# A transposed tile of the first FFN: one staging buffer, or the spent buffer of its other factor

## The chip, the cores and the metric

The kernel runs on one core of a Trainium2 chip. A core has a matrix engine (TensorE, PE in the profile), VectorE (DVE), ScalarE (ACT), GpSimd (POOL) and SyncE (SP), which in this kernel only issues transfers. The engines run side by side, each through its own list of instructions in order, and wait for each other on semaphores. Transfers between the chip's main memory and the on-chip memory are done by 16 DMA engines; here they are issued by SP and, where the transfer adds to what lies in the buffer, by POOL. The metric is the time of the program on the device in microseconds, lower is better; a run here is one launch of the whole program.

## The reference

The program is one layer of a diffusion backbone: half-step SwiGLU feed-forward network (FFN), token mixing, second FFN, final norm. It takes 256 context tokens and 256 latent tokens of width 2048. The part in question is the first FFN, which both kinds of tokens pass:

```python
def half_step_ffn(x, mod, i, g, w_up, w_down):
    h = adaln(x, g, mod, i)
    a, b = jnp.split(h @ w_up, 2, axis=-1)
    return x + 0.5 * mod[:, i + 2, None, :] * ((jax.nn.silu(a) * b) @ w_down)
```

`silu(a) * b` is the gated hidden activation. It is 5632 wide and is computed in blocks of 512 columns.

## The kernel before

**Precision.** Products are made of three matmuls: each fp32 operand is split into a rounded half `hi` (ScalarE, line 128) and a remainder `lo` (VectorE, line 129), and `mm3` (line 152) multiplies hi by hi, lo by hi and hi by lo. Weights arrive as 1 MB tiles, 128 x 2048, each split in two halves of 1024 columns. There are four `hi` and four `lo` buffers, so at most two weight tiles stand ready ahead of TensorE.

**Blocks.** The 11 blocks of hidden columns (`NB` is 11) are numbered 0 to 10. Block 0 is done differently and is not touched. Blocks 1 to 10 are each done by one call of `quad(n)`, which is a product of 2 x 2 sub-matrices with seven products instead of eight (`order`, m = 0 to 6). Each product takes two weight tiles, q = 0 and 1: 14 steps to a block, 24 matmuls to a step. Weight tiles lie in `chain_[0]` and `chain_[1]`, which stay and to which POOL adds the next summand by an accumulating transfer (line 740), or in the three `raw` buffers, which SP loads.

**Gating.** A block makes four gated tiles of 128 x 512 fp32 (256 KB). For tokens s = 0 (context) and 1 (latent):

- `p1` and `c11` (m = 0, 1) put silu of the first factor into `ca[s]`; `ca` has two buffers.
- `kept` (line 872, m = 2) copies a partial sum from PSUM into `cy[s]`, two buffers; `p35` (line 876, m = 3) does so into `cb[s]`, tag `c12`, two buffers.
- `c12` (m = 4) completes `cb[s]`, multiplies `ca[s]` by it and appends the tile to the list `turn`.
- `c22` (m = 5) completes `cy[s]` and takes a new `ca[s]`; `c21` (m = 6) does silu in it, multiplies by `cy[s]` and appends that tile to `turn`.

So each product has two factors in two buffers: the result stands in `ca[s]`, and the other factor, in `cb[s]` or `cy[s]`, is not read again.

**Turning.** `turned()` takes one tile from the list `turn`: VectorE transposes it in blocks of 32 x 32 (line 842) from `ca` into the tile `stg` of the pool `chp`, of which there is one buffer, and SP stores `stg` to main memory, `hidd[n]` (line 844). It is called once in each m, after the first group of matmuls of q = 0. Tiles of m = 4 are thus turned in m = 5 and 6 of the same block, tiles of m = 6 in m = 0 and 1 of the next.

**The order.** The framework places the instructions on their engines with a planner that estimates times and frees buffers; instructions marked with `keep_in_program_order`, such as the transposes through `pinned`, keep the order in which they are written. Semaphore waits are put in by the framework. A new tile in a buffer waits for all readers of the old one, stores among them.

**Beside it.** A stream of conditioning weights (`side`) runs through VectorE in the same loop: 512 KB tiles `sraw`, two buffers, loaded by SP and reduced on VectorE (line 208) against vectors in `cBh`. `cBh` is loaded anew once on the way (line 203).

**The change of stage.** After block 10 the remaining tiles are turned. The pool `f1u`, which holds `cBh`, `sraw`, `ca`, `cy` and `c12`, closes, and `f1` opens in its place with the accumulator `acc`. The down-projection runs in `pair(p)`, p = 0 to 4, again with seven products. Its first results are copied by ScalarE from PSUM into `acc` (line 1078). The last tile, (10, 3), is not turned at once: `turned` puts it into `last_turn`, and `pair(0)` turns it in its second step (line 1152). Block 10 is read back only by the last pair. Later, `last1` uses the same buffer `stg` of `chp` for another purpose (line 1222).

Of the kernel before, what the change touches and what calls it, by code (L numbers as in the profile page):

```python
# [9 lines left out]
F32 = mybir.dt.float32  # L10
# [9 lines left out]
P = 128  # L20
# [26 lines left out]
CB = 512  # L47
# [11 lines left out]
def tile_layer(ctx: ExitStack, tc: tile.TileContext, I: dict, out: bass.AP):  # L59
    nc = tc.nc  # L60
# [12 lines left out]
    def bank():  # L73
        return ps["mm"].tile([P, 512], F32, tag="mm", name="mm")

    def tbank():
        return ps["tr"].tile([P, 512], F32, tag="tr", name="tr")
# [38 lines left out]
    def raw_tile(n=2048):  # L116
        t = wp.tile([P, 2048], F32, tag="raw", name="raw", bufs=3)
        return t if n == 2048 else t[:, :n]

    def split(raw, n=2048):  # L120

        half = n // 2
        parts = []
        for h in range(2):
            hi = wp.tile([P, 1024], F32R, tag="hi", name="hi", bufs=4)[:, :half]
            lo = wp.tile([P, 1024], F32R, tag="lo", name="lo", bufs=4)[:, :half]
            src = raw[:, h * half : (h + 1) * half]
            scalar[0].activation(hi, src, AF.Copy)  # L128
            vector[0].tensor_tensor(lo, src, hi.bitcast(F32), op=ALU.subtract)  # L129
            parts.append((hi, lo))  # L130

        def at(w):
            h, o = divmod(w.start, half)
            return tuple(x[:, o : o + w.stop - w.start] for x in parts[h])

        return at
# [11 lines left out]
    def mm3(out_ap, sh, sl, mh, ml, first, last, skip=False, still=False):  # L148

        rest = ((sh, ml), (sl, mh)) if still else ((sl, mh), (sh, ml))  # L150
        for n, (s, m) in enumerate(((sh, mh), *rest)):
            tensor[0].matmul(out_ap, s, m, start=first and not n, stop=last and n == 2, skip_group_check=skip)  # L152
# [541 lines left out]
    hidd = [dr.tile([4, P, CB] if n else [P, 16, P], F32, name=f"hid{n}") for n in range(NF // FB)]  # L694
# [18 lines left out]
    def pinned(ins):  # L713
        tc.keep_in_program_order(ins)
# [22 lines left out]
    chp = chcm.__enter__()  # L737
# [3 lines left out]
    with pool(name="f1u", bufs=1) as f1u:  # L741
# [7 lines left out]
        def ca_tile():  # L749
            return f1u.tile([P, CB], F32, tag="ca", name="ca", bufs=2)  # L750
# [9 lines left out]
        def part(n, ab, c):  # L760
            return I["w_up1b"][n - 1, ab, c]

        def first_chain(n, c):
            nc.sync.dma_start(chain_[c], part(n, 0, c))
# [64 lines left out]
        forms = token_forms()  # L829
        steps(forms, 2)  # L830
        turn = []
        last_turn = []

        def turned():

            if not turn:
                return
            n, t, ca = turn.pop(0)

            def staged():  # L840
                stg = chp.tile([P, CB], F32, tag="stg", name="stg")
                pinned(nc.vector.transpose(stg, ca))
                s, tt = divmod(t, 2)
                nc.sync.dma_start(hidd[n][2 * tt + s], stg)

            if (n, t) == (NB - 1, 3):
                last_turn.append(staged)
            else:
                staged()

        add = lambda o, x, y: nc.vector.tensor_tensor(o, x, y, op=ALU.add)
        negative = lambda o, y: nc.vector.scalar_tensor_tensor(o, o, -1.0, y, op0=ALU.mult, op1=ALU.mult)
# [1 line left out]
        def c12_tile():  # L854
            return f1u.tile([P, CB], F32, tag="c12", name="c12", bufs=2)

        def quad(n, after=lambda step: None):

            X, Y, Z = {}, {}, {}
            ca, cy, cb, ra = {}, {}, {}, {}  # L860

            def p1(s):
                ca[s] = ca_tile()
                nc.scalar.activation(ca[s], X[s], AF.Copy)

            def c11(s):
                add(ca[s], Z[s], ca[s])
                nc.scalar.activation(ca[s], ca[s], AF.Silu)

            def kept(s):  # L870
                cy[s] = f1u.tile([P, CB], F32, tag="cy", name="cy", bufs=2)
                nc.scalar.activation(cy[s], Y[s], AF.Copy)

            def p35(s):
                cb[s] = c12_tile()
                nc.scalar.activation(cb[s], Y[s], AF.Copy)

            def c12(s):
                add(cb[s], X[s], cb[s])
                negative(ca[s], cb[s])  # L880
                turn.append((n, 2 * s, ca[s]))

            def c22(s):
                add(cy[s], X[s], cy[s])
                ca[s] = ca_tile()
                nc.scalar.activation(ca[s], X[s], AF.Copy)

            def c21(s):
                add(ca[s], Y[s], ca[s])
                nc.scalar.activation(ca[s], ca[s], AF.Silu)  # L890
                negative(ca[s], cy[s])
                turn.append((n, 2 * s + 1, ca[s]))

            def chained(ab, c):
                return lambda q: accum(chain_[q], part(n, ab, c + q))

            def again(q):
                if n + 1 < NB:
                    first_chain(n + 1, q)
                else:  # L900
                    nc.sync.dma_start(chain_[q], I["w_dn1"][0, 2 * q])

            def loaded(q):
                ra[q] = raw_tile()
                nc.sync.dma_start(ra[q], part(n, 1, 2 + q))
                return ra[q]

            def plain(q):
                r = raw_tile()
                nc.sync.dma_start(r, part(n, 0, 2 + q))  # L910
                return r

            held = lambda q: chain_[q]
            order = (
                (a11, held, X, True, chained(1, 0), p1),
                (a12, plain, Z, True, None, c11),
                (n1, held, Y, True, chained(1, 2), kept),
                (s4, loaded, Y, False, lambda q: accum(ra[q], part(n, 1, q)), p35),
                (s2, held, X, False, chained(0, 2), c12),
                (s3, lambda q: ra[q], X, False, None, c22),  # L920
                (a22, held, Y, True, again, c21),
            )
            for m, (a, src, dst, fresh, then, use) in enumerate(order):
                if fresh:
                    dst.update({s: bank() for s in range(2)})
                for q in range(2):
                    wt = split(src(q))
                    if then:
                        then(q)
                    after(2 * m + q)  # L930
                    for s in range(2):
                        for j in range(4):
                            k = 4 * q + j
                            hi, lo = a[0][:, s, k, :], a[1][:, s, k, :]
                            mm3(dst[s], hi, lo, *wt(slice(j * CB, (j + 1) * CB)), fresh and k == 0, k == 7, True)
                        if q and use:
                            use(s)
                        elif not s:
                            turned()
# [123 lines left out]
    def pair(p):  # L1063
# [5 lines left out]
        def added():  # L1069

            while residuals:
                accum(*residuals.pop(0))
# [71 lines left out]
        for m, (g, src, dst, fresh, then, use) in enumerate(order):  # L1144
            a = place0[m] if p == 0 and m < 2 else place[g]
            for c in range(2):
                wt = split(src(c))
                if then:
                    then(c)
                added()  # L1150
                if p == 0 and 2 * m + c == 1:
                    last_turn.pop()()
                for x in todo.get(2 * m + c, "").split():
                    if x.startswith("raw"):
                        hid_load(2 * p + 2 + int(x[3]), raws[int(x[3])])
                    else:
                        make[x]()
                if p == NP - 1:
                    if (2 * m + c) in GATES:
                        ahead.append(both_gates(GATES[2 * m + c]))  # L1160
                    if 2 * m + c == 13:
                        last_gate(0)
                        last_gate(1)
                    if m in (1, 4, 6):
                        gates = used[c] = ahead.pop(0)
                    elif m == 5:
                        gates = used[c]
                for s in range(2):
                    if fresh:
                        dst[c, s] = tbank() if c and dst is not X else bank()  # L1170
                    for j in range(FB):
                        k = slice((2 * j + s) * P, (2 * j + s + 1) * P)
                        mm3(dst[c, s], a[:, 0, k], a[:, 1, k], *wt(slice(j * CB, (j + 1) * CB)), fresh and j == 0, j == FB - 1, True)
                    use(c, s)
# [92 lines left out]
    with ExitStack() as mx:  # L1267
# [626 lines left out]
        for cb in range(NCB):  # L1894
# [8 lines left out]
            c = slice(cb * CB, (cb + 1) * CB)  # L1903
# [36 lines left out]
    with f2x:  # L1940
# [108 lines left out]
        turn = []  # L2049
# [393 lines left out]
```

## Time and profile before

| | |
|---|---|
| median of 3 runs | 2603.3 us (2600.16 to 2604.68) |
| the profiled execution, its own time | 2598.59 us |
| its span | 2596.9 us |
| its mean granted TensorE clock | 0.993 |
| first FFN, blocks 1 to 10 of the up-projection | about 164 to 944 us of the span |
| transposes into `stg` | 40, from 209.1 to 943.7 us |
| stores of `stg` | 40 of 256 KB, median 6.4 us from issue to landing |
| DMA traffic over the span | 684.69 MB, mean 264 GB/s |

Times in the profile count from the start of the span. A group is named by line, engine and operation, then `out<-in` by the program's names; in brackets stands how long the engine was idle before an instruction and what ended that. Matmuls overlap, so the pace of TensorE is read from the starts of successive matmuls and not from their durations. The granted clock is the share of full speed that TensorE was allowed. The DMA share is the mean busy share of the 16 DMA engines; by the way it is counted it can come out slightly above 1.

### The profile page before, as it was taken

The page shows a single profiled execution, that of the slowest core. Times are in us where ns is not written, and L with a number is a line of the kernel's source. Part 1 is how long each engine was busy: PE and PEld are TensorE (multiplying, and loading weights), DVE is VectorE, ACT ScalarE, POOL GpSimd, SP SyncE. Part 2 cuts the span into 40 slices and gives each one's busy share as a digit, 9 for nine tenths or more (in the row PEclk, how much of TensorE's full clock was granted, in tenths as well). Part 3 has the DMA queues.
Part 4 walks back from the last instruction along what each step waited for, and adds up shares of the span by engine and source line. Part 5 has one row for each costly group of instructions (what it writes and reads, how often), then busy time and mean ns, then how long its engine had stood idle before and what let it go on. Part 6 is the DMA issues. An engine that isn't in the chain of part 4 may idle for free. (4 is left out here: it accounts for less than half of the span.)

```text
span 2596.9 us, 33840 instructions
## 1 busy us (share of the span) xinstructions
PE 2559.5 (99%) x12486; PEld 2126.6 (82%) x12486; DVE 2205.3 (85%) x2924; ACT 1404.3 (54%) x1798; POOL 222.0 (9%) x271
## 2 busy tenths in 40 slices
PE   8999999999999999999999999999999999999998
PEld 5788888878887878888889989888898888888886
DVE  7789888878888788888887899798889888888987
ACT  4454444444444455444454448456476676666763
POOL 0000000100000100000110000120000000000001
PEclk8999999999999999999999999999999999999999
DMA  9889999999999989999986897776768999999985
GB/s 395 348 217 276 267 284 277 263 269 279 264 290 269 263 239 243 212 221 233 225 256 256 292 328 241 241 277 218 266 230 248 275 272 279 285 282 279 272 250 167
DMA packets 153477, 684.69 MB, mean 264 GB/s; under 512 B 22872, under 2 KB 43864, under 8 KB 92000
## 3 DMA queue, kind: packets, MB, share of 16 engines
q1 hardware_dynamic: 123936, 490.64, 51.5%
q0 software_dynamic: 29376, 191.90, 37.2%
q8 instruction: 98, 1.61, 0.2%
q14 instruction: 67, 0.55, 0.1%
HBM read 664.59 MB, written 17.89 MB: 263 GB/s over the span
## 5 line engine op out<-in xcount | busy, mean ns | idle before, releaser
L128 ACT ACTIVATE hi<-raw 128x1024 fp32r<-128x1024 f32 (+2 forms) x488 | 504.3, 1040 | 401.7 <-PE mm L152 304.1
L129 DVE TENSOR_TENSOR lo<-raw,hi 128x1024 fp32r<-128x1024 f32 (+2 forms) x476 | 566.4, 1202 | 109.6 <-ACT hi L128 91.4
L128 ACT ACTIVATE hi<-chain 128x1024 fp32r<-128x1024 f32 x352 | 369.9, 1059 | 351.6 <-PE mm L152 200.4
L129 DVE TENSOR_TENSOR lo<-chain,hi 128x1024 fp32r<-128x1024 f32 x352 | 424.4, 1218 | 88.8 <-ACT hi L128 78.9
L152 PE MATMUL mm<-lo,hhi 128*128 128x512 f32 (+3 forms) x1024 | 388.3, 379 | 6.4 <-DVE lo L129 6.3
L152 PE MATMUL mm<-hi,hhi 128*128 128x512 f32 (+3 forms) x1024 | 390.9, 382 | 0.0
L152 PE MATMUL mm<-hi,hlo 128*128 128x512 f32 (+3 forms) x1024 | 387.1, 378 | 0.0
L208 DVE SCALAR_TENSOR_TENSOR junk<-sraw,cBh 128x1024 fp8e5<-128x1024 f32 x192 | 234.1, 1219 | 38.1 <-DMA sraw<-in_w_mt 36.3
L152 PEld LDWEIGHTS mm<-lo,hhi 128*128 128x128 f32 x1024 | 193.1, 189 | 42.2 <-DVE lo L129 8.7
L152 PEld LDWEIGHTS mm<-hi,hlo 128*128 128x128 f32 x1024 | 193.3, 189 | 32.2
L152 PEld LDWEIGHTS mm<-hi,hhi 128*128 128x128 f32 x1024 | 193.3, 189 | 31.8
L129 DVE TENSOR_TENSOR lo<-ra,hi 128x1024 fp32r<-128x1024 f32 x104 | 126.0, 1221 | 25.7 <-ACT hi L128 22.0
L128 ACT ACTIVATE hi<-ra 128x1024 fp32r<-128x1024 f32 x104 | 110.0, 1061 | 65.7 <-PE mm L152 39.7
L152 PE MATMUL mm<-lo,hid2h 128*128 128x512 f32 x352 | 137.1, 390 | 0.1
L152 PE MATMUL mm<-hi,hid2h 128*128 128x512 f32 x352 | 137.0, 389 | 0.0
L152 PE MATMUL mm<-hi,hid2l 128*128 128x512 f32 x352 | 137.0, 389 | 0.0
L152 PE MATMUL mm<-hi,sumshl 128*128 128x512 f32 x400 | 123.2, 389 | 0.0
L740 POOL DMA_DIRECT2D chain<-in_w_up1b x60 | 53.1, 886 | 734.2 <-DVE lo L129 573.8
L208 DVE SCALAR_TENSOR_TENSOR sr<-sr,cBl 128x1024 f32<-128x1024 f32 x84 | 102.1, 1223 | 14.0 <-DMA sr<-in_w_mt 13.1
L152 PE MATMUL mm<-hi,sumshh 128*128 128x512 f32 x352 | 108.9, 391 | 1.3 <-DVE acc L1080 1.3
L152 PE MATMUL mm<-hhi,hi 128*128 128x512 f32 (+1 forms) x288 | 101.4, 352 | 0.0
L152 PE MATMUL mm<-hhi,lo 128*128 128x512 f32 (+1 forms) x288 | 99.0, 344 | 0.0
(488 smaller groups left out, 5416.2 us busy)
## 6 DMA issues: line engine op xcount, KB each, us to landing
raw<-in_w_dn SPq DMA_DIRECT2D x70, 1024.0 KB, 9.8
chain<-in_w_up1b POOLq DMA_DIRECT2D x60, 1024.0 KB, 10.7
sraw<-in_w_mt SPq DMA_DIRECT2D x96, 512.0 KB, 8.5
sr<-in_w_mt SPq DMA_DIRECT2D x81, 512.0 KB, 5.5
raw<-in_w_up1b SPq DMA_DIRECT2D x40, 1024.0 KB, 9.1
mraw<-in_w_m SPq DMA_DIRECT2D x32, 1024.0 KB, 7.5
chain<-in_w_dn POOLq DMA_DIRECT2D x30, 1024.0 KB, 10.0
chain<-in_w_up2b POOLq DMA_DIRECT2D x28, 1024.0 KB, 10.5
```

Source lines behind the costliest of these rows:

```text
L128: scalar[0].activation(hi, src, AF.Copy)
L129: vector[0].tensor_tensor(lo, src, hi.bitcast(F32), op=ALU.subtract)
L152: tensor[0].matmul(out_ap, s, m, start=first and not n, stop=last and n == 2, skip_group_check=skip)
L208: ins = nc.vector.scalar_tensor_tensor(junk() if junk else raw, raw, 1.0, cB[s], op0=ALU.mult, op1=ALU.mult, accum_out=mT[:, i, s, kt, h : ...
L740: accum = lambda dst, src: nc.gpsimd.dma_start(dst, src, accum_op=ALU.add)
```

## The change

The transposed tile goes into the buffer of the other factor of its product, `cb[s]` for tiles 0 and 2 of a block and `cy[s]` for tiles 1 and 3, and is stored from there. `turn` holds that buffer as a fourth entry. Only the very last tile, (10, 3), still goes into `stg`; it is turned with the others at the end of block 10, and `last_turn` and its place in `pair(0)` are gone.

```diff
         turn = []
-        last_turn = []

         def turned():

             if not turn:
                 return
-            n, t, ca = turn.pop(0)
-
-            def staged():
-                stg = chp.tile([P, CB], F32, tag="stg", name="stg")
-                pinned(nc.vector.transpose(stg, ca))
-                s, tt = divmod(t, 2)
-                nc.sync.dma_start(hidd[n][2 * tt + s], stg)
-
+            n, t, ca, spare = turn.pop(0)
             if (n, t) == (NB - 1, 3):
-                last_turn.append(staged)
-            else:
-                staged()
+                spare = chp.tile([P, CB], F32, tag="stg", name="stg")
+            pinned(nc.vector.transpose(spare, ca))
+            s, tt = divmod(t, 2)
+            nc.sync.dma_start(hidd[n][2 * tt + s], spare)
...
             def c12(s):
                 add(cb[s], X[s], cb[s])
                 negative(ca[s], cb[s])
-                turn.append((n, 2 * s, ca[s]))
+                turn.append((n, 2 * s, ca[s], cb[s]))
...
                 negative(ca[s], cy[s])
-                turn.append((n, 2 * s + 1, ca[s]))
+                turn.append((n, 2 * s + 1, ca[s], cy[s]))
...
                 added()
-                if p == 0 and 2 * m + c == 1:
-                    last_turn.pop()()
                 for x in todo.get(2 * m + c, "").split():
```

## The prediction

> **What bounds the kernel now.** I read the busy times of the engines first, then the busy times in stretches of one pass of the loop over blocks.
>
> ```profile
> PE 2559.5 (99%) x12486; PEld 2126.6 (82%) x12486; DVE 2205.3 (85%) x2924; ACT 1404.3 (54%) x1798; POOL 222.0 (9%) x271
> ```
>
> TensorE is the bound as a whole: 37 us of the 2596.9 us span are idle. A change that only frees VectorE can pay only where TensorE now stops. To find such places I cut the first FFN's up-projection at the first copy into `cy` of each block (line 872), so that each stretch holds the same 336 matmuls. The columns are the length, then busy time and count of PE, PEld, DVE, ACT and POOL, the granted TensorE clock, the DMA share and GB/s.
>
> ```profile
> 185.91:262.07 76.16, 76.16 (x337) 63.06 (x336) 64.56 (x81) 35.99 (x41) 7.01 (x9) 1.00 0.99 266
> ...
> 492.22:575.78 83.56, 79.54 (x337) 64.95 (x336) 64.97 (x83) 35.69 (x41) 7.23 (x9) 0.96 0.96 265
> 575.78:651.94 76.16, 76.16 (x337) 63.08 (x336) 65.83 (x87) 35.83 (x41) 6.88 (x8) 1.00 0.98 273
> ...
> 728.35:804.96 76.61, 76.50 (x337) 62.94 (x336) 65.96 (x90) 35.37 (x41) 7.06 (x8) 1.00 0.97 278
> 804.96:885.68 80.72, 77.90 (x337) 64.05 (x336) 70.72 (x92) 36.03 (x41) 7.22 (x9) 0.98 0.99 272
> 885.68:961.00 75.32, 69.99 (x304) 56.23 (x302) 56.32 (x69) 39.90 (x45) 5.11 (x6) 1.00 0.89 236
> ```
>
> An undisturbed block takes 76.16 us, which is 0.2267 us for each of its 336 matmuls, and most blocks take just that. One block is 7.4 us longer, one 4.6 us, and the last stretch, where the up-projection gives way to the down-projection, has idle time too. The question is which of these stops the staging tile causes. The view of the instructions that touch `stg` answers for all 40 transposes.
>
> ```profile
> L842 DVE STREAM_TRANSPOSE stg<-ca x40: 690/702/712, 209.1 to 943.7; 128x512 f32<-128x512 f32 x40
> ...
>   DMA hid<-stg: 16.0, 4
> ...
>   ACT ca L864: 22.4, 8
> ...
> DMA to landing us min/median/max: 2.3/6.4/12.5
> ```
>
> Only 4 of the 40 transposes find the tile still being stored, 16.0 us in all. The longest of the four stands in VectorE's order of time (start, duration, idle time before in brackets):
>
> ```profile
> 546.62 2.35 DVE L129 TENSOR_TENSOR lo<-raw,hi 128x1024 fp32r<-128x1024 f32 x2
> 557.65 0.71 DVE L842 STREAM_TRANSPOSE stg<-ca 128x512 f32<-128x512 f32 x1 [8.69 <-DMA hid<-stg]
> 558.29 2.31 DVE L129 TENSOR_TENSOR lo<-raw,hi 128x1024 fp32r<-128x1024 f32 x2
> ```
>
> VectorE stood for 8.69 us, and the `lo` halves of the next weights stood behind it. ScalarE was ready for them and then stopped too, because line 864 wants the `ca` buffer that this transpose reads:
>
> ```profile
> 549.90 1.06 ACT L128 ACTIVATE hi<-raw 128x1024 fp32r<-128x1024 f32 x1 [0.25 <-PE mm L152]
> 558.46 0.60 ACT L864 ACTIVATE ca<-mm 128x512 f32<-128x512 f32 x1 [7.50 <-DVE stg L842]
> 558.95 1.99 ACT L128 ACTIVATE hi<-chain 128x1024 fp32r<-128x1024 f32 x2
> ```
>
> TensorE ran out of `lo` (13 matmuls of the same length stand between 559.52 and 565.24, left out but for the first):
>
> ```profile
> 555.59 0.39 PE L152 MATMUL mm<-hi,hlo 128*128 128x512 f32 x1
> 559.52 0.80 PE L152 MATMUL mm<-lo,hhi 128*128 128x512 f32 x1 [3.54 <-DVE lo L129]
> 560.12 0.63 PE L152 MATMUL mm<-hi,hhi 128*128 128x512 f32 x1
> ...
> 565.24 0.50 PE L152 MATMUL mm<-hi,hhi 128*128 128x512 f32 x1
> 565.58 0.39 PE L152 MATMUL mm<-hi,hlo 128*128 128x512 f32 x1
> ```
>
> The store was slow because the scheduled reload of `cBh` was issued just ahead of it on SP; its last part took 13.2 us to land, the store 12.5 us, and the accumulating load of `chain` that POOL issued behind them 10.6 us (three landings, in this order, at the end of the fence):
>
> ```profile
> 542.44 0.49 SPq L203 DMA_DIRECT2D cBh<-ccd  x1
> ...
> 545.02 0.33 SPq L844 DMA_DIRECT2D hid<-stg  x1
> ...
> 546.50 0.89 POOL L740 DMA_DIRECT2D chain<-in_w_up1b  x1 [6.08 <-DVE lo L129]
> ...
> DMA to landing us min/median/max: 13.2/13.2/13.2
> ...
> DMA to landing us min/median/max: 12.5/12.5/12.5
> ...
> DMA to landing us min/median/max: 10.6/10.6/10.6
> ```
>
> **The change, part by part.** *Instructions.* There are 40 transposes of 0.70 us and 40 stores of 256 KB before and after; only the buffer differs. Nothing is saved in work.
>
> *The wait that goes, in the block from 492.22.* From 555.59 to 565.58 TensorE began 15 matmuls in 9.99 us; undisturbed they take 15 x 0.2267 = 3.40 us. The stop cost 6.59 us: about 3.70 us of gap, and 2.9 us at the half clock behind it. In the new kernel this transpose has an own buffer, so it can start when the `lo` at 546.62 ends, at 548.97. What is late next? Both `hi` halves were done by 550.96, so `lo` is ready by about 552.2, and TensorE wants it at 555.8. The following weights sit in `chain`, whose later half landed at 546.5 + 10.6 = 557.1; at full pace TensorE reaches it 48 matmuls after 555.4, at 566.3, and a `hi` and a `lo` cost 1.06 + 1.2 us for each half of it, so the first is ready by about 559.5. I take the whole 6.59 us. The other 0.8 us of that block's 7.4 us was lost before 555 and stays.
>
> On the clock, the Trainium skill, "TensorE: Matmul & The Clock Gate", Part 1, says that full rate is withdrawn after an idle window of about 3.4 us and given back after a busy one of the same length. By that figure the slow part would be some 1.7 us, an estimate, and the stop 5.4 us; the rows here show 2.9 us and 6.59 us, so the rows are used.
>
> *The other three waits* are 16.0 - 8.7 = 7.3 us together. One falls in the long block itself, ahead of its stop; one in the block from 728.35. VectorE is busy only 65 of 76 us in a block, and TensorE holds two steps of finished weights, so these two are worth nothing, at most the 0.4 us that the block from 728.35 is over 76.16. The last stands in the change of stage:
>
> ```profile
> 938.94 0.70 DVE L842 STREAM_TRANSPOSE stg<-ca 128x512 f32<-128x512 f32 x1
> ...
> 943.72 0.71 DVE L842 STREAM_TRANSPOSE stg<-ca 128x512 f32<-128x512 f32 x1 [1.83 <-DMA hid<-stg]
> ...
> 944.52 1.58 ACT L1078 ACTIVATE acc<-mm 128x512 f32<-128x512 f32 x3 [4.32 <-issue]
> ...
> 952.49 0.50 PE L152 MATMUL tr<-lo,hidl 128*128 128x512 f32 x1 [0.51 <-DVE lo L129]
> ...
> 961.18 1.84 PE L152 MATMUL tr<-hi,sumshh 128*128 128x512 f32 x4 [2.23 <-DVE acc L1080]
> ...
> DMA to landing us min/median/max: 4.0/4.0/4.0
> ```
>
> *The transpose that is moved.* That of the last tile (943.72) now stands right behind its neighbour of 938.94, into `stg`, with nothing to wait for. It and its store move past the `lo` instructions and past SP's loads of `w_dn1` that stood between; each of these is put back by 0.63 us or by one issue of 0.33 us, and the 1.83 us go. TensorE may be short of a `lo` by as much, 0.63 us, which the later stops at 952 and 961 absorb: where it waits anyway, it arrives later and waits less.
>
> *The wait that is added, here.* The 4.32 us of idle time before ScalarE's first copy into `acc` ends 0.1 us after the transpose at 943.72 ends (944.42). `acc` takes the memory of the closed pool that holds `ca`, `cy` and `c12`, so I read that gap as a wait for the last reader of that pool. The new last reader is the store from `cy` of the neighbour tile, issued near 939.7. With its own landing time of now, 4.0 us, ScalarE goes on at 943.7, 0.8 us sooner. With the least and the greatest of the 40 landings, 2.3 and 12.5 us, it would be 2.5 us sooner or 7.7 us later. Queued behind are the `hi` halves of the first down weights, and TensorE behind these. I take a gain of 0.8 us, because the trace has that very store.
>
> *The waits that are added in the loop.* Line 872 (`cy`) and line 876 (`c12`) on ScalarE now wait for a store; behind them stand `hi` halves for two steps. The shortest distance is that of the fourth tile to the second `cy`:
>
> ```profile
> 791.58 0.70 DVE L842 STREAM_TRANSPOSE stg<-ca 128x512 f32<-128x512 f32 x1
> ...
> 808.42 0.57 ACT L872 ACTIVATE cy<-mm 128x512 f32<-128x512 f32 x1
> ```
>
> The store goes out 0.7 us after the transpose starts; with the longest landing, 12.5 us, it is over at 804.8, which leaves 3.6 us. In the other blocks the distance is longer, and for `c12`, which is filled again a step of the order later, longer still. Cost: nothing, as long as no store takes over 16 us.
>
> **Sum.** 6.6 + 0.8 = 7.4 us. Against the profiled execution: 2596.9 us of span and 1.7 us around it, 2598.6 us, becomes 2591.2 us. That execution was 4.7 us below the median of the three timed ones, 2603.3 us, and I carry the difference over: 2595.9, say 2596 us.
>
> **Rivals.**
>
> *A. The transfers take it back* (2600 us). The stop also let the DMA engines catch up:
>
> ```profile
> 558.00:561.00 3.00, 1.48 (x4) 1.19 (x5) 3.00 (x4) 2.49 (x3) 0.00 (x0) 0.61 0.65 268
> ```
>
> The slow block has 0.96 x 83.56 = 80.2 us of DMA busy time, with 1 MB for `cBh` more than others. If that is real occupation, the block can't take less than 80.2 us, and 3.4 us are won instead of 6.6 us: about 2600 us. Against it: in the next block ScalarE's `hi` waits for TensorE, not for data.
>
> ```profile
> 582.35 1.06 ACT L128 ACTIVATE hi<-chain 128x1024 fp32r<-128x1024 f32 x1 [2.53 <-PE mm L152]
> ```
>
> The Trainium skill, "Trainium Kernel Development and Optimization", Key Constraints, supports this rival: transfers issued by SP and by POOL run on the same 16 engines and interleave, so issuing the next loads 8 us sooner does not widen anything.
>
> *B. The seam gets a longer wait than it loses* (2607 us). This is the case that ends slower. The place is ScalarE's first copy into `acc`. It decides from a landing of 4.8 us on (939.7 to 944.5). At 12.5 us ScalarE is 7.7 us late, TensorE starves as long and adds 2.9 us at the half clock as it did at 559.52: 10.6 us, less the 6.6 us won, gives +4.0 us. For it: the median store takes 6.4 us, and two stores now go out together. Against it: this one took 4.0 us.
>
> *C. The wait only changes its name* (2603 us). The order on each engine is set by a planner from its own estimates, and with other waits it may set the seven transposes, the `lo` and the `cy` copies differently, so that a stop of the same size appears elsewhere.
>
> *D. More is won* (2591 us). The other long block loses its time to a late `sraw`, with this stop of TensorE:
>
> ```profile
> 821.80 0.80 PE L152 MATMUL mm<-lo,s2h 128*128 128x512 f32 x1 [2.82 <-DVE lo L129]
> ```
>
> The change doesn't touch it, but transfers shifted by 7 us may meet differently; then its 4.6 us go as well.
>
> **How the numbers follow.** Forecast 0.45, A 0.20, C 0.13, B 0.12, D 0.10. The likeliest is 2596 us, its own range 2592 to 2600 us. The whole range goes from D with the early landing at the seam, 2590 us, to B, 2607 us; what is left out is a store slower than any seen, or a planner that does worse than C. A measurement of this kernel can tell about 0.2%, 5.2 us, from no change: below 2598.1 us is faster, above 2608.5 us slower. Faster: nine tenths of the forecast and D, 0.50. Slower: half of B and a little of C, 0.08. The same: 0.42.
>
> **What would show it.** Right: no transpose with idle time put down to a store; the fifth stretch at about 77 us with the granted clock at 1.00; line 864's longest wait well below 7.50 us; stores still 40. Wrong: the fifth stretch at 80 us or more with `hi` waiting for `chain` (A); the first copy into `acc` later than 945 us less what was won before (B); a new releaser of `cy` (line 872) that is a store; or other blocks longer than 76.2 us that were not before (C).

## The result, and the profile after

| | before | after |
|---|---|---|
| median on the device | 2601.53 us (8 runs, 2596.1 to 2604.68) | 2591.34 us (8 runs, 2586.2 to 2595.07) |
| ratio, 95% interval | | 0.9962 (0.9951 to 0.9972) |
| profiled execution, its own time | 2598.59 us | 2588.91 us |
| its span | 2596.9 us | 2587.2 us |
| its granted TensorE clock | 0.993 | 0.995 |

The changed kernel is faster by 0.38%, which is 9.9 us of 2601.5 us, with an interval of 7.3 to 12.7 us. The forecast was a gain of 7.4 us, and a time of 2596 us.

**Where the time went.** The up-projection of the changed kernel, cut in the same way as before, at the first copy into `cy` of each block (now line 865), in stretches of 336 matmuls. The columns are those of the prediction's second fence: length, busy time of PE, PEld, DVE, ACT and POOL, granted clock, DMA share, GB/s.

```profile
491.18:567.76 76.58, 76.58 (x337) 62.83 (x336) 64.71 (x82) 35.91 (x41) 7.23 (x9) 1.00 0.99 281
567.76:643.92 76.16, 76.16 (x337) 63.06 (x336) 65.87 (x87) 35.81 (x40) 6.88 (x8) 1.00 0.99 278
...
720.51:796.67 76.16, 76.16 (x337) 63.06 (x336) 66.75 (x92) 35.50 (x41) 7.06 (x8) 1.00 0.98 282
796.67:876.66 79.99, 78.05 (x337) 64.14 (x336) 70.12 (x90) 35.91 (x40) 7.23 (x9) 0.98 0.99 273
```

The fifth stretch took 83.56 us before and takes 76.58 us now; its clock rose from 0.96 to 1.00, and TensorE is busy for all of it. The next stretch still takes the undisturbed 76.16 us, so nothing was pushed into it. The stretch from 796.67 is long as before (80.72 us then). The account of the whole span, from the two traces: 0.8 us were won before block 1 reached its first copy, 7.0 us in the fifth stretch, 1.2 us in the other stretches together, 2.3 us between the last of these copies and the first product of the down-projection with `sumshl` (983.9 us before, 972.6 us now), and 1.6 us were lost again later, which makes the 9.7 us between the spans.

**Who waits for the stores.** This is the view of the stores of the changed kernel (duration of the issue in ns: least, median, greatest; first and last start):

```profile
L842 SPq DMA_DIRECT2D hid<-c x20: 326/327/1792, 209.1 to 923.2; - x20
L842 SPq DMA_DIRECT2D hid<-cy x19: 320/327/403, 234.6 to 931.1; - x19
...
  ACT acc L1071: 2.1, 1
...
DMA to landing us min/median/max: 3.7/7.6/12.5
```

39 of the 40 stores go out of the factors' buffers, the last one (at 931.73 us) out of `stg`. The traces hold the landing of only 32 of the 40 stores, before and after, so every least, median and greatest landing given for them, ahead of the prediction and in it too, is that of 32. The stores did not become quicker, the median rose from 6.4 to 7.6 us. But in place of four transposes only one instruction waits for any of them: ScalarE's first copy into `acc`, for 2.1 us. No copy into `cy` or `c12` does. The store that held up VectorE before is just as slow in the new trace; the landing of tile (5, 1):

```profile
DMA to landing us min/median/max: 12.5/12.5/12.5
```

The transpose of tile (5, 3) in VectorE's order of time, then ScalarE's instruction behind it:

```profile
545.21 2.35 DVE L129 TENSOR_TENSOR lo<-raw,hi 128x1024 fp32r<-128x1024 f32 x2
547.48 0.70 DVE L840 STREAM_TRANSPOSE cy<-ca 128x512 f32<-128x512 f32 x1
```

```profile
549.46 0.58 ACT L857 ACTIVATE ca<-mm 128x512 f32<-128x512 f32 x1
```

There is no bracket behind either: the 8.69 us of VectorE and the 7.50 us of ScalarE behind it are gone. ScalarE's list of waits in the up-projection still has a row for this pair (total, times, longest), first before, then after:

```profile
ACT ca L864 <- DVE stg L842: 22.4, 8, 7.5
```

```profile
ACT ca L857 <- DVE cy L840: 14.7, 7, 5.8
ACT cy L865 <- PE mm L152: 12.9, 9, 1.8
```

ScalarE still waits for transposes, up to 5.8 us, but no stop of TensorE follows them: the longest ends at 784.24 us, and the only stops of TensorE that the profile shows in these blocks, 1.94 us at 812.62 and 1.77 us at 915.57, wait for VectorE's `lo`. And the copy into `cy` waits for TensorE alone.

**The change of stage.** VectorE's first instruction of the new stage, one stop of TensorE, and the window from the first product of the down-projection with `hidh` to the first with `sumshl`, in the kernel before (start, duration, idle time before in brackets; the window's columns as above):

```profile
945.46 1.22 DVE L1006 TENSOR_TENSOR v<-hidl,hidh 128x1024 f32<-128x1024 f32 x1
...
957.71 1.24 PE L152 MATMUL mm<-hi,sumshh 128*128 128x512 f32 x4 [1.31 <-DVE acc L1080]
...
933.50:983.90 50.40, 46.36 (x194) 36.55 (x193) 37.44 (x38) 30.29 (x37) 6.19 (x7) 0.97 0.90 205
```

and in the changed one VectorE, ScalarE's first copy into `acc`, TensorE's two stops, the landing of the store of (10, 1), and the same window:

```profile
930.40 0.70 DVE L840 STREAM_TRANSPOSE cy<-ca 128x512 f32<-128x512 f32 x1
931.03 0.67 DVE L840 STREAM_TRANSPOSE stg<-ca 128x512 f32<-128x512 f32 x1
...
934.96 1.23 DVE L999 TENSOR_TENSOR v<-hidl,hidh 128x1024 f32<-128x1024 f32 x1 [1.01 <-issue]
...
935.03 1.09 ACT L1071 ACTIVATE acc<-mm 128x512 f32<-128x512 f32 x2 [2.10 <-DMA hid<-cy]
...
950.84 1.24 PE L152 MATMUL tr<-hi,sumshh 128*128 128x512 f32 x4 [1.62 <-DVE acc L1073]
952.48 0.51 PE L152 MATMUL mm<-lo,sumshh 128*128 128x512 f32 x1 [0.40 <-DVE lo L129]
...
DMA to landing us min/median/max: 3.7/3.7/3.7
...
926.40:972.60 46.20, 44.18 (x194) 35.83 (x193) 36.00 (x36) 29.75 (x36) 6.19 (x7) 1.00 0.93 212
```

Counted from the first copy into `cy` of block 10 (885.68 and 876.66 us), the first copy into `acc` comes at 58.84 us before and 58.37 us after, 0.5 us sooner. VectorE's first `v` comes at 59.78 and 58.30 us, 1.5 us sooner. TensorE's stops for VectorE in the window were 0.51 (952.49), 1.31 and 2.23 us (961.18) before, 4.05 us together; now they are 1.62 and 0.40 us, 2.02 us together. The whole window is 4.1 us shorter: 2.0 us are these stops, and the other 2.1 us go with the granted clock, which was 0.97 in it and is 1.00 now. Ahead of the window, from the first copy into `cy` of block 10 on, the changed kernel lost 1.9 us (49.74 us at a clock of 0.97 behind a stop of 1.77 us, where it had been 47.85 us at 1.00). That leaves the 2.3 us. Which stops the slower clock follows differs from trace to trace, as the last section shows, so this split belongs to these two traces.

### The profile page after: what moved, and what is told of

It is laid out like the page before. It is cut to its first block, busy times and chain, and to the rows that moved or that the text cites. A ratio compares the mean times of both kernels' runs of the same rounds, so it can differ in the third digit from the quotient of the medians.

```text
span 2587.2 us, 33868 instructions
## 1 busy us (share of the span) xinstructions
PE 2555.3 (99%) x12486; PEld 2124.7 (82%) x12486; DVE 2206.6 (85%) x2924; ACT 1405.5 (54%) x1798; POOL 221.9 (9%) x271
```

## The experiments

Each variant was timed in five rounds beside the kernel before on the same chip. e1 to e4 ran with 30 runs of the kernel before (median 2600.36 us), e5 to e8 with 21 (2600.06 us). Ratios are against these; the gains in us are worked out from them.

**e1: only the one transpose.** The kernel before, with tile (5, 3) alone turned into its `cy`; all other tiles go through `stg`.

```diff
-            n, t, ca = turn.pop(0)
+            n, t, ca, spare = turn.pop(0)
...
-                stg = chp.tile([P, CB], F32, tag="stg", name="stg")
+                stg = spare if (n, t) == (5, 3) else chp.tile([P, CB], F32, tag="stg", name="stg")
...
-                turn.append((n, 2 * s, ca[s]))
+                turn.append((n, 2 * s, ca[s], cb[s]))
...
-                turn.append((n, 2 * s + 1, ca[s]))
+                turn.append((n, 2 * s + 1, ca[s], cy[s]))
```

> The kernel before with a single tile changed: (5, 3), whose transpose stood 8.69 us, goes into its cy buffer; the other 39 go through stg as before. Theory (the gain is one stop, made by the reload of cBh): block 5's stretch falls from 83.6 us to about 76.6 us and the time by 6 to 7 us, ratio to before about 0.9975. Rival (the gain is spread over all 40 tiles and their waits on ScalarE): a fortieth of it shows, ratio within 0.0005 of 1.

Measured: 2594.82 us, ratio 0.9983 (0.9972 to 0.9995), a gain of 4.4 us (1.3 to 7.3). The window of the fifth stretch, and the transpose:

```profile
495.00:571.10 76.10, 76.10 (x337) 63.04 (x336) 64.17 (x81) 35.78 (x40) 7.20 (x9) 1.00 1.00 285
```

```profile
550.46 0.70 DVE L842 STREAM_TRANSPOSE cy<-ca 128x512 f32<-128x512 f32 x1
```

The stretch takes 76.16 us between its two copies and the wait is gone. One buffer for one tile in 40 removes the whole stop, 7.4 us in the trace; by the timed runs it is worth less than that, the interval ends at 7.3 us. The profiled execution as a whole was hardly shorter than that of the kernel before (2598.16 against 2598.59 us): its third stretch took 78.61 us, where it had been 76.18, and from the first copy into `cy` of block 10 to the first product with `sumshl` it took 101.6 us, where it had been 98.2. Whether that is the edit's doing or the spread between executions, one trace can't tell.

**e2: everything but that.** The changed kernel, with tiles (5, 1) and (5, 3) again through `stg`.

```diff
-            if (n, t) == (NB - 1, 3):
+            if (n, t) in ((5, 1), (5, 3), (NB - 1, 3)):
```

> The changed kernel with only tiles (5, 1) and (5, 3) put back through stg, so that the one pair around the reload of cBh waits as before. Theory: a stop of 6 to 7 us comes back at the third transpose after 540 us; the rest of the gain, about 3 us, stays: ratio to before 0.998 to 1.000. Rival (spread gain): the gain stays nearly whole, ratio 0.996 to 0.9965.

Measured: 2598.86 us, ratio 0.999 (0.9977 to 1.0003), a gain of 2.6 us that can't be told from none. The fifth stretch, VectorE and TensorE in it:

```profile
492.00:574.40 82.40, 78.10 (x337) 63.94 (x336) 65.08 (x83) 35.66 (x40) 7.19 (x9) 0.98 0.96 269
```

```profile
557.66 0.71 DVE L840 STREAM_TRANSPOSE stg<-ca 128x512 f32<-128x512 f32 x1 [8.66 <-DMA hid<-stg]
```

```profile
559.53 0.80 PE L152 MATMUL mm<-lo,hhi 128*128 128x512 f32 x1 [3.54 <-DVE lo L129]
```

With these two tiles the wait is back, 8.66 us where it was 8.69, with the same gap of 3.54 us on TensorE. So most of the gain hangs on this pair of tiles. What stays is what 37 other tiles and the change of stage bring, and it is not clear of nothing.

**e3: only the change of stage.** The kernel before, with block 10 as in the changed kernel: its first three tiles into their factors' buffers, the last one into `stg` at once.

```diff
-                stg = chp.tile([P, CB], F32, tag="stg", name="stg")
+                stg = spare if n == NB - 1 and t < 3 else chp.tile([P, CB], F32, tag="stg", name="stg")
...
-            if (n, t) == (NB - 1, 3):
-                last_turn.append(staged)
-            else:
-                staged()
+            staged()
...
-                if p == 0 and 2 * m + c == 1:
-                    last_turn.pop()()
```

> The kernel before with only block 10 as in the changed kernel: its tiles 0, 1 and 2 into cb and cy, the last one into stg at once, no last_turn. Theory: the 1.83 us wait of VectorE goes, ScalarE's first copy into acc waits for a store instead; gain 0.5 to 1 us, ratio 0.9995 to 1.000. Rival (the change of stage holds a good part of the gain): 3 us, ratio 0.9985 to 0.999.

Measured: 2598.32 us, ratio 0.9989 (0.9978 to 0.9999), a gain of 2.9 us (0.3 to 5.7). The fifth stretch (81.99 us between its two copies), VectorE in it, and the first copy into `acc`:

```profile
495.40:577.40 82.00, 78.40 (x337) 64.05 (x336) 64.67 (x82) 35.71 (x41) 7.23 (x9) 0.98 0.97 271
```

```profile
560.39 0.71 DVE L841 STREAM_TRANSPOSE stg<-ca 128x512 f32<-128x512 f32 x1 [8.58 <-DMA hid<-stg]
```

```profile
943.23 1.09 ACT L1074 ACTIVATE acc<-mm 128x512 f32<-128x512 f32 x2 [3.60 <-issue]
```

The median gain of this part is larger than the 0.8 us that the prediction gave it, but the interval has 0.8 us inside. e1 and e3 together make 7.3 us, the changed kernel 9.9 us; with intervals of about 3 us on each side that is no contradiction. To size this part I measured, in all traces, the time from the first product of the down-projection with `hidh` to the first with `sumshl`, which holds 192 matmuls (43.5 us at full pace). The old way takes 50.3 us (before), 49.0 (e1) and 51.5 (e4), mean 50.3; the new way 46.2 (after), 47.9 (e2), 48.7 (e3), 49.1 (e7) and 49.5 (e8), mean 48.3. (With the additional load of e5 and e6, which delays this part, it is 55.6 us the old way and 52.2 us the new way.) The difference is 2 us, and the single traces spread by as much or more, so that it is likely but not settled.

**e4: take away what made the store slow.** The kernel before without the second load of `cBh`. This leaves a part of the computation out: the second half of the conditioning sums is taken against the vectors of the first half.

```diff
-        cond = Conditions(lambda h: h, lambda h: conditions(halves, h, h + 1), lambda h: halves)
+        cond = Conditions(lambda h: h, lambda h: h or conditions(halves, h, h + 1), lambda h: halves)
```

> The kernel before without the second load of cBh: the second half of the conditioning sums for the gate of the first FFN and the second adaLN uses the vectors of the first half, so those sums are left wrong; the work of the engines is the same and 1 MB of transfers is left out. Theory (the store was slow because it ran beside that reload): the store of tile (5, 1) lands in 4 to 8 us, its successor waits under 1 us, block 5 takes 76.2 to 77 us and the time falls by 6 to 7 us, ratio 0.9975. Rival (the store is slow for another reason, such as the accumulating loads): the wait stays above 5 us, the time within 1 us.

Measured: 2591.74 us, ratio 0.9968 (0.9955 to 0.998), a gain of 8.3 us (5.2 to 11.7). The fifth stretch, the transpose of (5, 3), and the landing of the store of (5, 1):

```profile
491.60:567.90 76.30, 76.30 (x337) 62.96 (x336) 65.07 (x83) 35.80 (x40) 7.19 (x9) 1.00 0.98 276
```

```profile
548.30 0.71 DVE L842 STREAM_TRANSPOSE stg<-ca 128x512 f32<-128x512 f32 x1 [0.55 <-DMA hid<-stg]
```

```profile
DMA to landing us min/median/max: 4.4/4.4/4.4
```

Without the load in front of it the store lands in 4.4 us instead of 12.5 us, the wait shrinks to 0.55 us, and the stop is gone with the single staging tile still in use. So two things together made the stop: one buffer, and one load that made one store slow. In this trace seven transposes still wait for a store, up to 2.83 us, and TensorE has no stop longer than 0.55 us in blocks 1 to 9 up to the first copy of block 10.

**e5 and e6: a second such load.** Both kernels, with the vectors of the same half loaded once more two blocks later, at item 67 of the conditioning stream. Nothing that is computed changes, but the stream also runs three steps later from there on.

```diff
-            if cB.half(h) != half:
+            if cB.half(h) != half or n == 67:
```

> The kernel before with the reload of cBh made a second time, with the same vectors, two blocks later and at the same place in a block, right ahead of the store of tile (7, 1); the conditioning stream then runs three steps later to its end. Theory (such a reload beside the single staging tile makes the stop): the transpose of tile (7, 3) stands 6 to 9 us for a store, the seventh stretch between first cy copies (76.4 us before) grows to 82 to 84 us, the time rises by 5 to 8 us, ratio 1.002 to 1.003. Rival (the stop of block 5 was something else): no such wait, ratio within 0.001 of 1.

> The changed kernel with the same additional reload of cBh. Theory: the store from cy is just as slow, 10 to 13 us, but nobody waits for it: the seventh stretch stays at 76.2 to 77.5 us, and the time stays within 2 us of the changed kernel, ratio to before 0.996 to 0.997. Rival (the transfers themselves take the time back): the stretch grows by 3 us or more, ratio 0.997 to 0.998.

Measured: e5 (the kernel before with it) 2624.76 us, ratio 1.0103 (1.0084 to 1.0121); e6 (the changed kernel with it) 2617.3 us, ratio 1.0065 (1.0052 to 1.0079). The seventh stretch of e5, with VectorE, TensorE and the landing of the store:

```profile
651.80:733.80 82.00, 78.23 (x339) 64.16 (x338) 64.04 (x85) 35.74 (x40) 7.18 (x9) 0.98 0.96 266
```

```profile
716.91 0.71 DVE L842 STREAM_TRANSPOSE stg<-ca 128x512 f32<-128x512 f32 x1 [9.82 <-DMA hid<-stg]
```

```profile
718.78 0.80 PE L152 MATMUL mm<-lo,hhi 128*128 128x512 f32 x1 [3.77 <-DVE lo L129]
```

```profile
DMA to landing us min/median/max: 14.8/14.8/14.8
```

and the same of e6:

```profile
649.50:727.10 77.60, 77.11 (x339) 62.84 (x338) 64.63 (x86) 35.55 (x40) 7.19 (x9) 1.00 0.99 281
```

```profile
706.27 0.70 DVE L840 STREAM_TRANSPOSE cy<-ca 128x512 f32<-128x512 f32 x1
```

```profile
DMA to landing us min/median/max: 14.5/14.5/14.5
```

In the stretch itself the two do nearly what was expected: the load makes a second stop of the same kind, 82.05 us between the copies, where there is a single staging tile, and with the factors' buffers the stretch takes 77.65 us although its store is as slow. Fifth and seventh stretch together differ by 9.6 us between e5 and e6 (the fifth takes 78.23 us in e6, with two stops of TensorE of 0.46 and 0.99 us and no transpose that waits). The timed runs of the two differ by 7.5 us in their medians and by 0.0038 in their ratios, 9.9 us. That is no more than the changed kernel gains without the load, so the second stop is shown by the traces; the timed runs do not show a price for it.

The totals missed by far: the edit cost the kernel before 24.7 us and the changed kernel about 26 us. Most of that comes after the loop. From the first copy into `cy` of block 10 to the first product with `sumshl` it is 107.0 us in e5 (98.2 us before) and 103.1 us in e6 (95.9 us after); in e5 it is then 472.8 us from that product (994.6 us) to the first gate of the token mixer (1467.4 us), where the kernel before takes 454.1 us (983.9 to 1438.0 us). I had priced the load where it stands and not what its delay does to the conditioning stream, which ends later: in e6 its last instruction starts at 948.30 us, 66.8 us behind the first copy of block 10, in the changed kernel at 921.14 us, 44.5 us behind it, and the last two transposes stand behind it on VectorE. What it meets after the change of stage was not followed.

**e7: how much room the loop has.** The changed kernel, with the stores from `cy` written one product later in blocks 1 to 9.

```diff
+        held_back = []
...
+            while held_back:
+                nc.sync.dma_start(*held_back.pop())
...
-            nc.sync.dma_start(hidd[n][2 * tt + s], spare)
+            if t % 2 and n < NB - 1:
+                held_back.append((hidd[n][2 * tt + s], spare))
+            else:
+                nc.sync.dma_start(hidd[n][2 * tt + s], spare)
```

> The changed kernel with the stores of tiles 1 and 3 of blocks 1 to 9, those that lie in cy, issued one product (10.9 us) later on SP, so that the new wait of ScalarE's cy copy gets that much less room. Theory (the added wait is free with some 16 to 20 us from transpose to copy): with about 9 us left and stores of 4 to 12 us, the copy of the second cy waits for a store in a few of the blocks, up to 4 us each, and the two steps of finished weights cover most of it: 0 to 6 us slower than the changed kernel, ratio to before 0.996 to 0.9985. Rival (the room is plenty): no wait for a store at all, ratio 0.996.

Measured: 2593.12 us, ratio 0.9968 (0.9958 to 0.9978), the same as the changed kernel within the intervals. The copies into `cy` (line 871 here) and what they waited for, and one transpose on VectorE with its store on SP:

```profile
L871 ACT ACTIVATE cy<-mm x20: 576/581/600, 185.0 to 878.2; 128x512 f32<-128x512 f32 x20
...
  PE mm L152: 10.7, 8
...
773.07 0.70 DVE L843 STREAM_TRANSPOSE cy<-ca 128x512 f32<-128x512 f32 x1
...
773.80 0.33 SPq L837 DMA_DIRECT2D hid<-cy  x1
```

The edit did not do what it was meant to do. Of the 18 stores that were written one product (10.9 us) later, 17 were issued 0.72 to 0.73 us after the start of their transpose, as in the changed kernel, and one 3.49 us after it. The stores are not marked to keep their order, so I take it that the planner put them back; that is not shown. e7 therefore repeats the changed kernel and says nothing about room. The traces do: from the landing of a store out of `cy` to the next copy into that buffer, the least time is 8.4 us in the changed kernel (issued at 784.18, landed 7.6 us later, copy at 800.1 us) and 7.4 us in e7, by the landings that are recorded. So no copy waits for a store, but a store issued 10.9 us later would not have fitted there.

**e8: is it the tile or the pool?** The changed kernel with `acc` as four tiles of 128 x 2048 instead of one, so that the first copies need less of the closed pool's memory.

```diff
-    acc = f1.tile([P, 4, D], F32, name="acc", bufs=1)
+    accs = [f1.tile([P, D], F32, name=f"acc{t}", bufs=1) for t in range(4)]
...
-    col = lambda t, cb: acc[:, t, cb * CB : (cb + 1) * CB]
+    col = lambda t, cb: accs[t][:, cb * CB : (cb + 1) * CB]
```

> The changed kernel with acc as four tiles of 128 x 2048 in the same memory instead of one tile, so that only the quarter that lies over cy waits for its store; instructions and order are the same. Theory A (the first copy into acc is what the change of stage waits for, as the prediction took it): the 2.1 us wait of ScalarE for hid<-cy goes and 1 to 2 us are won, ratio 0.9955. Theory B (VectorE, busy without a pause there, sets the pace): the wait goes and the time stays, ratio 0.996 to 0.9965.

Measured: 2592.42 us, ratio 0.997 (0.9958 to 0.9981), the same as the changed kernel. The store of (10, 1) on SP, then VectorE's and ScalarE's first instructions in the new pool:

```profile
934.28 0.33 SPq L842 DMA_DIRECT2D hid<-cy  x1
```

```profile
938.41 1.23 DVE L999 TENSOR_TENSOR v<-hidl,hidh 128x1024 f32<-128x1024 f32 x1 [1.32 <-issue]
```

```profile
938.48 1.09 ACT L1071 ACTIVATE acc<-mm 128x512 f32<-128x512 f32 x2 [3.67 <-issue]
```

The edit did not take the wait away. Two engines' first writes into two different tiles of the new pool start within 0.1 us of each other, 4.1 us after that store was issued and 0.1 us after it landed (4.04 us). It is the same in all six traces with the new way, after, e2, e3 and e6 to e8: `v` starts 0.08 to 0.19 us and the copy into `acc` 0.15 to 0.26 us after the landing of that store. So both wait for it, also where the profile calls the wait "issue". I read this as a wait for the closed pool as a whole, whatever tile lies over which; no run has put that to the test. What the change of stage would take without that wait therefore stays open.

## Why the prediction was right, and where it was off

- **The stop in the block from 492.22, 6.6 us: right.** In the trace the stretch became 6.98 us shorter. e1 removes the stop alone (76.16 us), e2 puts it back alone (82.47 us), e4 removes it from the other side, by removing the load that made the store slow, and e5 makes a second one by adding such a load. What would be late next, the `chain` weights, was not: TensorE is busy for the whole stretch.
- **The other waits in the loop, worth nothing: right as far as it can be seen.** The stretch of the one in the block from 728.35 went from 76.61 to 76.16 us, but the stretches 2 to 4 and 6 to 8 differ by up to 4 us between traces of kernels that do the same there.
- **The change of stage, 0.8 us: right in sign, probably too small.** It measured 2 us by the means of the traces and 2.9 us (0.3 to 5.7) by e3, so 0.8 us is not excluded. The step that was probably mis-sized is "I take a gain of 0.8 us, because the trace has that very store". The store did land as thought (3.7 us) and the copy into `acc` did come 0.5 us sooner. But the profile puts TensorE's stops there down to VectorE's adds into `acc` and its `lo`, not to that copy. VectorE was rid of the 1.83 us ahead of the transpose, and its `v` came 1.5 us sooner. The prediction had the 1.83 us and two of these stops in its rows, but took its price from ScalarE's copy and let the stops only absorb a delay, where they became 2.0 us shorter. It also did not see that `v` on VectorE would wait for the same store.
- **The waits added in the loop, nothing: right.** No copy into `cy` or `c12` waits for a store; the least room between a recorded landing and the copy into `cy` is 8.4 us in the changed kernel. No run has used that room up.
- **The sum.** 7.4 us forecast, 9.9 us measured (7.3 to 12.7): the forecast lies just inside the interval. The change of stage may account for 1 to 2 us of the difference; it is not settled. The time, 2591.34 us, is 0.7 us below the range of 2592 to 2600 us that went with the forecast, and it is where D was put. That it falls on D's number is chance, for D did not happen; 1.8 us of the distance to 2596 us come from the kernel before, whose median is 2601.5 us in eight runs where it was 2603.3 us in three.
- **A, the transfers take it back: did not happen.** The stretch takes 76.58 us with a DMA share of 0.99, less than the 80.2 us of DMA busy time that the rival held for its floor, and the next one 76.16 us. Worked out as length by rate, it moves 21.5 MB now (76.58 us at 281 GB/s) and moved 22.1 MB before (83.56 us at 265 GB/s), so 0.6 MB less does not account for it (at the old busy time per MB, 21.5 MB would be 78 us): the busy time of the slow block was no floor.
- **B, a longer wait at the seam: did not happen,** and its mechanism is there. ScalarE's copy into `acc` does wait for the store of the neighbour tile, 2.10 us, as was thought; this store landed in 3.7 us, below the 4.8 us from which the rival decides, and in 4.0 to 4.4 us in e2, e3, e7 and e8. In e6, which issued it later, it landed in 6.9 us: ScalarE's copy waited 6.08 us and VectorE's `v` 4.27 us for it, and a stop of TensorE of 4.08 us followed. So the longer wait that the rival feared can come up.
- **C, the wait changes its name: did not happen.** No other block became longer by more than 0.3 us.
- **D, the other long block gets well too: not by this change.** That block still took 79.99 us. Its stop depends on when a conditioning tile lands; by the traces of all kernels it cost between 0.6 us (e7) and 4.6 us (before), whatever was changed. That is one reason why the single traces differ as they do, and probably the timed runs too.

## What to carry to other kernels

A staging tile with one buffer is not slow by the sum of its waits. Of 40 transposes four waited, and only one of them stopped the engine that sets the time for long (the one at the change of stage probably cost 2 us); look for the one store that a bigger transfer was issued ahead of, and ask there what TensorE runs out of. A spent buffer of the same shape is a second staging buffer for nothing where its next use lies further off than the longest store, and that distance is to be measured against the slowest landing in the trace, not the median. Where a stage begins, price a change by the engine that the bound engine waits for there, and not by the first wait that one meets.

## What the hardware showed beyond that

**Half clock after a short gap.** In the changed kernel TensorE stopped for only 1.77 us, and the clock went down behind it. TensorE in order of time, and the window (columns as above):

```profile
915.57 0.50 PE L152 MATMUL mm<-lo,hhi 128*128 128x512 f32 x1 [1.77 <-DVE lo L129]
...
916.69 0.63 PE L152 MATMUL mm<-hi,hhi 128*128 128x512 f32 x1
...
919.25 0.63 PE L152 MATMUL mm<-hi,hhi 128*128 128x512 f32 x1
```

```profile
916.00:920.00 4.00, 4.00 (x12) 3.10 (x11) 4.00 (x10) 0.00 (x0) 0.00 (x0) 0.57 0.75 274
```

Six matmuls further on, 2.56 us have gone by, 0.427 us for each where 0.2267 us is the full pace, and the granted clock of the window is 0.57. The Trainium skill, "TensorE: Matmul & The Clock Gate", Part 1, has the clock halved after an idle window of about 3.4 us; here just over half of that was enough. The length alone does not decide, though. In e4 a stop of 2.33 us at nearly the same place left the pace as it was, six matmuls in 1.37 us:

```profile
915.27 0.50 PE L152 MATMUL mm<-lo,hhi 128*128 128x512 f32 x1 [2.33 <-DVE lo L129]
...
916.30 0.40 PE L152 MATMUL mm<-hi,hhi 128*128 128x512 f32 x1
...
917.67 0.39 PE L152 MATMUL mm<-hi,hhi 128*128 128x512 f32 x1
```

Stops of 2.25 us in e2 (959.41 us), 2.37 us in e7 (915.88 us) and 2.36 us in e8 (918.83 us) were not followed by a slower clock either: it is 1.00 in the 4 us behind each. The recorded changes of the clock lie whole multiples of 3.413 us apart in a trace (814.07 and 916.47 us in that of the changed kernel are 30 of them apart), so it may matter how a stop lies across such a stretch; no run has tested that. In this kernel, then, a gap of 2 us can cost more than itself, and stops that look too short to matter are worth a look.

**How long a small store takes.** A store of 256 KB landed in 2.3 to 12.5 us in the kernel before, and the one behind the load of the conditioning vectors in 12.4 to 14.8 us in all nine kernels that have that load, against 4.4 us without it (e4). Here the size said little about such a time; what was issued ahead of it said more.
